# A recurrent block in one planned order on all engines, with eight single-bank PSUM tiles and sigmoids by halves

## The chip, the cores and the metric

The kernel runs on one core of one Trainium2 chip. A core has TensorE (PE in the profile), VectorE (DVE), ScalarE (ACT), GpSimd (POOL) and SyncE (SP), each with a queue of its own that is worked off in order, and 16 DMA engines. SBUF is its working memory; PSUM, which PE writes, is used in banks of 512 float32 for each of 128 partitions, eight in all. The metric is the device time of one execution in microseconds, taken as the median of several runs. A profile records one further execution.

## The reference

One layer of a Griffin-like recurrent block and one of stick-breaking attention, each followed by a SwiGLU feed-forward, on 1024 positions of width 1024. The change touches the recurrent block and the first matmuls after it:

```python
u = jnp.einsum("bsd,de->bse", x, w_in) + b_in
gate_branch, rec = u[..., :LRU_WIDTH], u[..., LRU_WIDTH:]
rec = causal_depthwise_conv(rec, conv_w, conv_b)
gl = jnp.einsum("bsnc,gncd->gbsnd", rec_blk, gate_w).reshape(2, bsz, seq, LRU_WIDTH)
r_gate = jax.nn.sigmoid(gl[0])
i_gate = jax.nn.sigmoid(gl[1])
log_a = -LRU_C * r_gate * jax.nn.softplus(-lam)
a = jnp.exp(log_a)
mult = jnp.sqrt(-jnp.expm1(2.0 * log_a))
b = mult * (i_gate * rec)
_, h = lax.associative_scan(_linear_recurrence_combine, (a, b), axis=1)
y = jax.nn.gelu(gate_branch, approximate=True) * h
return jnp.einsum("bse,ed->bsd", y, w_out) + b_out
```

## The kernel before

Channels lie on partitions, positions in the free dimension, in two halves `n` of 512. Each float32 operand is split into a high and a low part, and each product is three matmuls of 128x128 by 128x512 (`mm3`, L127: high-high, high-low, low-high). A column of `w_in` is one tile of 128 output channels: 8 row tiles times 3 matmuls times 2 halves, 48 matmuls. The recurrent branch has columns A0 to A7, the gate branch B0 to B7, and the gates come in pairs of columns, G0 to G3: for each of two columns and two gates 2 halves of 6 matmuls, again 48.

*The start* (L248 to L323) loads the first four columns in pieces of one row tile (`fr[k]`) beside the input `x` (`xr[k][n]`) and the table of constants `vc`. For each row tile ACT makes the high part of the weights (`fh`) and of the scaled input (`xh`), DVE the low parts (`fl`, `xl`), and PE does half 0 of all four columns `FIRST`. Eight small matmuls on an identity come ahead of them. Then PE does the second halves (`second`, L305), and between them the statistics of the RMSNorm: `column_stats` (L192) sums squares by matmul into one spare bank, DVE and ACT make `rcol`, and `spread` (L172) broadcasts it through the same bank, from where DVE copies it to `rbc[n]`.

*The block* (L326 to L480). A (`stage_a`, L396): DVE scales the column by `rbc` into `u`, ACT applies the newest tap, DVE three more (`rec`), ACT and DVE split the result (`rh`, `rl`). G (`stage_g`, L412): gate matmuls on `rh` and `rl`, then on ACT sigmoids, tanh, exp, sqrt and a copy, and on DVE products and the scan into `ys[e]`. B (`stage_b`, L443): scaling and GELU. Y (L451): `ys[e]` times the GELU. `softplus(-lam)` is a chain of small DVE instructions on 8 elements (L332 to L355). `last_tile` (L455) does column B7, splits all `ys` into `xh` and `xl`, and loads the first tiles of `w_out`. Weights arrive as 512 KB (`raw`, three buffers), ACT copies the high part (`whi`), DVE subtracts the low part (`wlo`).

PSUM is four tiles of two banks (`psl`, two pools). The order of PE in the block is written out by the string of stages; the other engines are ordered there by the framework's scheduler (`manual_schedule` names PE alone, L472). At the start and in the feed-forward the order of every engine is that of the code, but that the scheduler sets the small softplus instructions in between. After the block PE does the output projection (`mix_out_ffn_in`, L541), 16 groups of 24 matmuls into `ob_ps`, in a pool of six single-bank tiles.

## Time and profile before

| what | value |
|---|---|
| median of three runs | 2217.38 us (2214.4 to 2218.05) |
| the profiled execution | 2218.56 us, span 2216.8 |
| PE busy, 0 to 240 us | 229.29 us |
| PE busy, 240 to 300 us | 59.81 us |
| first feed-forward matmul | 330.31 us |

A row of a list by waits reads: engine, tile and line that waited, what ended the wait, time in total, times, longest. A row of a timeline: start, duration, engine, line, operation, output <- inputs, and in brackets the idle time before it. PE's matmuls are pipelined: what counts is how far apart they start, not how long each lasts. A row of a list of windows: the stretch, its length, busy time and count for PE, PE's weight loads, DVE, ACT and POOL, then the granted clock of PE (1.00 is full speed), the share of the DMA engines and GB/s.

### The profile page before, as it was taken

What the parts mean: (1) busy time and instruction counts of PE and PEld (TensorE: products, weight loads), DVE (VectorE), ACT (ScalarE), POOL (GpSimd) and SP (SyncE); (2) the same over time, 40 slices, a digit from 0 to 9 for tenths busy, and PEclk for the clock granted to TensorE, in tenths of its full rate; (3) what the DMA queues carried; (4) which work ended last, traced back from release to release, by engine and by line L of the source; (5) the groups of instructions that cost most, each with busy time, mean ns of one, the idle gap of its engine ahead of it and who ended that gap; (6) DMA issues with size and microseconds to landing.
All of it is one profiled execution on the core that took longest, in us unless ns stands there. A gap on an engine that the chain in (4) does not pass through costs nothing.

```text
span 2216.8 us, 28236 instructions
## 1 busy us (share of the span) xinstructions
PE 2177.2 (98%) x10050; PEld 1805.3 (81%) x10050; DVE 1721.9 (78%) x2412; ACT 1152.7 (52%) x2033; POOL 224.1 (10%) x356
## 2 busy tenths in 40 slices
PE   9899999999999999999999999999999999999997
PEld 7788888888888888878888888878888888888886
DVE  7877778677777887868888888866876777788886
ACT  5657545344444544646666666653534444454455
POOL 0000020000000000003333333421000000000001
PEclk9999999999999999999999999989999999999998
DMA  4021312334444864453333333631133444466442
GB/s 172 10 67 48 124 38 72 105 119 157 143 155 131 278 192 122 145 143 86 88 94 97 104 86 105 186 125 61 46 106 120 152 147 146 145 237 228 126 145 86
DMA packets 132316, 273.50 MB, mean 123 GB/s; under 512 B 15312, under 2 KB 22608, under 8 KB 132176
## 3 DMA queue, kind: packets, MB, share of 16 engines
q1 hardware_dynamic: 131600, 270.86, 38.9%
q8 instruction: 79, 1.29, 0.2%
q10 hardware_dynamic: 576, 0.85, 0.1%
q14 instruction: 61, 0.50, 0.1%
HBM read 175.70 MB, written 70.78 MB: 111 GB/s over the span
## 4 chain that ended last, share of the span: by engine, by line
PE 83%; DVE 9%; ACT 4%; DMA 2%; issue 1%; SPq 1%; DVEq 0%; ACTq 0%
PE p_ps L130 18%; PE p_ps L128 18%; PE p_ps L129 18%; PE qk_ps L130 3%; PE qk_ps L128 2%; PE qk_ps L129 2%; PE ob_ps L129 2%; PE ob_ps L128 2%; PE ob_ps L130 2%; PE wt_ps L1454 2%; PE a_ps L130 2%; PE a_ps L128 2%; PE a_ps L129 2%; DVE F L1442 2%; PE z_ps L1417 1%
## 5 line engine op out<-in xcount | busy, mean ns | idle before, releaser
L1443 POOL TENSOR_TENSOR w<-w,F 128x128 f32<-128x128 f32 (+1 forms) x192 | 184.6, 962 | 314.9 <-DVE F L1440 176.1
L128 PE MATMUL p_ps<-vh,wbh 128*128 128x512 f32 x524 | 204.3, 390 | 2.0 <-ACT ta L1003 2.0
L130 PE MATMUL p_ps<-vh,wcl 128*128 128x512 f32 x524 | 204.2, 390 | 0.5 <-DVE wcl L630 0.5
L130 PE MATMUL p_ps<-vh,wbl 128*128 128x512 f32 x524 | 204.3, 390 | 0.0
L130 PE MATMUL p_ps<-vh,wal 128*128 128x512 f32 x524 | 204.1, 390 | 0.1
L128 PE MATMUL p_ps<-vh,wch 128*128 128x512 f32 x524 | 204.1, 390 | 0.0
L128 PE MATMUL p_ps<-vh,wah 128*128 128x512 f32 x524 | 203.9, 389 | 0.0
L129 PE MATMUL p_ps<-vl,wch 128*128 128x512 f32 x524 | 203.9, 389 | 0.0
L129 PE MATMUL p_ps<-vl,wbh 128*128 128x512 f32 x524 | 203.9, 389 | 0.0
L129 PE MATMUL p_ps<-vl,wah 128*128 128x512 f32 x524 | 203.9, 389 | 0.0
L616 ACT CAST wbh<-sb 128x1024 fp32r<-128x1024 f32 (+2 forms) x69 | 69.6, 1009 | 192.6 <-DVE sb L600 192.6
L1440 DVE TENSOR_TENSOR_SCAN F<-F,unit 128x128 f32<-128x128 f32 (+3 forms) x128 | 126.9, 992 | 5.4 <-ACT F L1436 5.4
L1463 ACT CAST th<-wt_ps 128x512 fp32r<-128x512 f32 x192 | 93.3, 486 | 71.8 <-PE wt_ps L1454 69.8
L1464 DVE TENSOR_TENSOR tl<-wt_ps,th 128x512 fp32r<-128x512 f32 x192 | 105.1, 548 | 28.9 <-ACT th L1463 27.8
L128 PE MATMUL qk_ps<-vh,whi 128*128 128x512 f32 x264 | 118.8, 450 | 0.6 <-ACT vh L208 0.6
L128 PEld LDWEIGHTS p_ps<-vh,wbh 128*128 128x128 f32 x524 | 98.4, 188 | 22.6 <-ACT ta L1003 2.5
L130 PEld LDWEIGHTS p_ps<-vh,wcl 128*128 128x128 f32 x524 | 98.4, 188 | 21.8 <-DVE wcl L630 1.4
L130 PEld LDWEIGHTS p_ps<-vh,wbl 128*128 128x128 f32 x524 | 98.4, 188 | 21.7 <-DVE wbl L620 1.3
L130 PEld LDWEIGHTS p_ps<-vh,wal 128*128 128x128 f32 x524 | 98.4, 188 | 21.4 <-DVE wal L611 1.0
L129 PEld LDWEIGHTS p_ps<-vl,wah 128*128 128x128 f32 x524 | 98.4, 188 | 20.3
L129 PEld LDWEIGHTS p_ps<-vl,wch 128*128 128x128 f32 x524 | 98.4, 188 | 20.3
L128 PEld LDWEIGHTS p_ps<-vh,wah 128*128 128x128 f32 x524 | 98.4, 188 | 20.3
(408 smaller groups left out, 5725.9 us busy)
## 6 DMA issues: line engine op xcount, KB each, us to landing
raw<-in_ffn_w_in SPq DMA_DIRECT2D x88, 512.0 KB, 3.8
vl<-pd SPq DMA_DIRECT2D x128, 256.0 KB, 3.7
pd<-U SPq DMA_DIRECT2D x90, 256.0 KB, 2.3
raw<-in_ffn_w_out SPq DMA_DIRECT2D x28, 512.0 KB, 4.1
raw<-in_attn_w_qkv SPq DMA_DIRECT2D x24, 512.0 KB, 3.6
acc<-pd SPq DMA_DIRECT2D x28, 256.0 KB, 2.6
pph<-rbc SPq DMA_DIRECT2D x28, 256.0 KB, 2.5
ppl<-acc SPq DMA_DIRECT2D x28, 256.0 KB, 2.6
```

The costliest lines, as they stand in the source:

```text
L128: nc.tensor.matmul(ps, lhsT=wh, rhs=mh, start=first, stop=False, **kw)
L129: nc.tensor.matmul(ps, lhsT=wh, rhs=ml, start=False, stop=False, **kw)
L130: nc.tensor.matmul(ps, lhsT=wl, rhs=mh, start=False, stop=last, **kw)
L616: nc.scalar.copy(self.full(self.wb), self.full(self.sb))
L1417: nc.tensor.matmul(ps[:, 0 : c1 - c0], lhsT=lhsT, rhs=KL[q][hx][:, c0:c1], start=False, stop=True)
L1440: nc.vector.tensor_tensor_scan(rev, rev, unit[:, NB - n :][:, ::-1], first, op0=ALU.mult, op1=ALU.add)
L1442: nc.vector.tensor_tensor_scan(rev, rev, rev, first, op0=ALU.mult, op1=ALU.bypass)
L1443: nc.gpsimd.tensor_mul(wt, wt, F[:, 1 : n + 1])
L1454: nc.tensor.transpose(tp[:, c : c + P], W[q, hx, j, kb // 4][:, (kb % 4) * P : (kb % 4 + 1) * P], ident)
L1463: nc.scalar.copy(th[:, q0:], tp[:, q0:])
L1464: nc.vector.tensor_sub(tl[:, q0:], tp[:, q0:], f32(th)[:, q0:])
```

## The change

The recurrent block is emitted by a planner. `lru_plan` enters every step as a task with engine, duration, predecessors and rank; `Plan.emit` always takes the task that can begin first by those durations (ties by rank), and emits it. PE, ACT, DVE and POOL then run in that order. The columns go in another order, PSUM is eight tiles of one bank taken in turn, each half of a column and each half of a gate has its own, and each sigmoid is two instructions of 512. `softplus` moves from the start into the block (`decay`). At the start the table goes first on SP's queue, `xr[0][0]` on ACT's, DVE makes `fh[0]`, there are ten small matmuls, and the second halves stand in whole columns between statistics and spreads. After the block the first four output groups do their first six row tiles, all four, before the last two of each.

```diff
-FIRST = (ND, ND + 1, 0, ND + 2)
+FIRST = (ND, ND + 1, ND + 2, 0)
+class Plan:
+    def __init__(self, **free):
+        self.tasks, self.free = [], free
+
+    def add(self, eng, us, fn, after=(), rank=0, table=None):
+        self.tasks.append((eng, us, fn, [a for a in after if a is not None], rank, table))
+        return len(self.tasks) - 1
+
+    def emit(self):
+        left, end, free, table = set(range(len(self.tasks))), {}, dict(self.free), {}
+        while left:
+            best = None
+            for i in left:
+                eng, us, _, after, rank, tab = self.tasks[i]
+                after[:] = [a if isinstance(a, int) else a[0][a[1]] for a in after]
+                if any(a not in end for a in after):
+                    continue
+                begin = max([free[eng], *(end[a] + (0.0 if self.tasks[a][0] == eng else 0.15) for a in after)])
+                if tab is not None and table.get(eng) != tab:
+                    begin += 1.3
+                key = (begin, rank, i)
+                if best is None or key < best:
+                    best = key
+            begin, _, i = best
+            eng, us, fn, _, _, tab = self.tasks[i]
+            free[eng] = end[i] = begin + us
+            if tab is not None:
+                table[eng] = tab
+            if eng == "dma":
+                free[eng], end[i] = begin + 0.5, begin + us
+            left.remove(i)
+            fn()
+def lru_plan(plan, order, fn):
+    col, rank = 5.44, {w: i for i, w in enumerate(order)}
+    last, end = f"B{ND - 1}", len(order)
+    wants = [w for w in order if w[0] != "Y"][len(FIRST):] + [last, "out0", "out1", "out2"]
+    soft = plan.add("dve", 3.6, fn["soft", 0], [], rank["G0"] - 1)
...
+    def weights(w):
+        i = wants.index(w)
+        r = rank.get(w, end) - 2.5
+        loads[i] = plan.add("dma", 2.6, fn["load", w], [los.get(i - 3), loads.get(i - 1)], r)
+        his[i] = plan.add("act", 1.05, fn["hi", w], [loads[i], his.get(i - 1), used.get(i - 3)], r)
+        los[i] = plan.add("dve", 1.16, fn["lo", w], [his[i]], r)
+        return los[i]
...
+            pe = plan.add("pe", us, fn[key, w, n], [pe, wt, *deps, *free[bank % 8]], r)
+            out.append((pe, bank % 8))
+            bank += 1
...
+    for s_, w in enumerate(order):
+        kind, e = w[0], int(w[1])
+        if kind == "Y":
+            Y[e] = plan.add("dve", 1.16, fn["y", e], [scan[e], gel[e], Y.get(e - 1)], s_ + 3)
+            continue
+        if s_ < len(FIRST):
+            pe = plan.add("pe", col, fn["first", w], [pe], s_)
+            parts = [(None, bank), (pe, bank + 1)]
+            bank += 2
+        else:
+            wt = weights(w)
+        if kind in "AB" and s_ >= len(FIRST):
+            parts = halves(w, wt, (), col, "pe", s_)
+            used[wants.index(w)] = pe
+        if kind == "A":
+            r = rank[f"G{e // 2}"] - 2
+            c = plan.add("dve", 0.1, fn["u", e], [taps.get(e - 2)], r)
+            m = multiply("um", e, parts, r, [c])
+            idn[e] = plan.add("act", 1.24, fn["id", e], [*m, (plus, e - 3) if e > 2 else None, idn.get(e - 1)], r)
+            t = idn[e]
+            for j in range(3):
+                t = plan.add("dve", 1.22, fn["tap", e, j], [t], r)
+            taps[e] = t
+            rh = plan.add("act", 1.05, fn["rh", e], [t, (gates, (e - 3) // 2) if e > 2 else None], r)
+            rl[e] = plan.add("dve", 1.16, fn["rl", e], [rh], r)
...
+                p = [halves((i, g), wt, (rl[2 * e], rl[2 * e + 1]), col / 4, "pg", s_) for g in range(2)]
+                sig = [[], []]
+                for g in range(2):
+                    for n, (q, b) in enumerate(p[g]):
+                        sig[g].append(
+                            plan.add("act", 0.62, fn["sig", i, g, n], [q, scan.get(i - 2), root.get(i - 2), plus.get(i - 2)], r, "sig")
+                        )
+                        free[b] = [sig[g][-1]]
+                ths.append((plan.add("act", 1.15, fn["th", i], [*sig[0], soft], r, "sig"), sig))
+            for i, (th, sig) in zip(pair, ths):
+                r = rank.get(f"Y{i}", end) - 1
+                sr = plan.add("dve", 1.16, fn["sr", i], sig[1], r)
+                t = plan.add("act", 1.15, fn["ex", i], [th], r, "exp")
+                for j in range(3):
+                    t = plan.add("dve", 1.16 if j == 0 else 1.22, fn["m", i, j], [t, sr], r)
+                root[i] = plan.add("act", 1.06, fn["sq", i], [t], r, "sqrt")
+                plus[i] = plan.add("act", 1.05, fn["a1", i], [t], r)
+                st = plan.add("dve", 1.16, fn["st", i], [root[i], sr], r)
+                scan[i] = plan.add("dve", 2.25, fn["scan", i], [st, plus[i]], r)
+                plus[i] = plan.add("act", 0.0, fn["none", 0], [sr, plus[i]], r)
+            used[wants.index(w)] = gates[e] = pe
...
+    turn = [0]
+
+    def ptile(name):
+        turn[0] += 1
+        return psl.tile([P, NB], F32, tag=f"a{(turn[0] - 1) % 8}", name=name)
+
+    pa = {j: [ptile("a_ps") for n in range(NH)] for j in FIRST}
...
-        nc.scalar.dma_start(f4(fr[0]), lru_first[0])
-        nc.scalar.dma_start(vc, table)
+        nc.scalar.dma_start(xr[0][0], x[0, 0])
+        nc.sync.dma_start(vc, table)
         for k in range(ND):
-            nc.sync.dma_start(xr[k][0], x[k, 0])
+            nc.sync.dma_start(f4(fr[k]), lru_first[k])
             if k:
-                nc.sync.dma_start(f4(fr[k]), lru_first[k])
+                nc.sync.dma_start(xr[k][0], x[k, 0])
...
-        for i in range(8):
+        bank = pa[FIRST[3]][1]
+        for i in range(10):
...
-            nc.scalar.copy(fh[k], fr[k])
+            (nc.scalar.copy if k else V.tensor_copy)(fh[k], fr[k])
...
         column_stats(sacc[0], bank, 0)
-        second(0, range(4))
+        second(0, range(ND))
         spread_to(0)
-        second(0, range(4, ND))
-        column_stats(sacc[1], bank, 1)
-        second(1, range(4))
-        spread_to(1)
-        second(1, range(4, ND))
-        second(2, range(ND))
-        second(3, range(ND))
...
+        column_stats(sacc[1], bank, 1)
+        second(1, range(ND))
+        spread_to(1)
+        second(2, range(ND))
+        second(3, range(ND))
...
+        def pe_gate(eg, n):
+            e, g = eg
+            b, c = e // 2, slice(e % 2 * P, (e % 2 + 1) * P)
+            gh, gl = W[f"G{b}"]
+            PS[eg, n] = ptile("g_ps")
+            for k in range(2):
+                q = 2 * b + k
+                mm3(
+                    PS[eg, n], gh[:, g, k, c], gl[:, g, k, c],
+                    half(rech[q], n), half(recl[q], n), k == 0, k == 1,
+                )
...
+        def gate(e, g, n):
+            if g == n == 0:
+                GA[e], GT_[e], GS[e] = wide("ga", 2), wide("gt", 2), wide("gs", 2)
+            nc.scalar.activation(
+                half((GA, GS)[g][e], n), PS[(e, g), n], AF.Sigmoid, bias=col(V_GB + g * ND, e)
+            )
...
-        with tc.manual_schedule(engines={E.PE}):
-            for what in "A0 A1 B0 A2 B1 G0 A3 Y0 Y1 A4 B2 G1 A5 Y2 A6 B3 Y3 G2 A7 B4 Y4 B5 G3 Y5 B6 Y6".split():
...
+        with tc.manual_schedule(engines={E.PE, E.Activation, E.DVE, E.Pool}):
+            plan = Plan(pe=31.2, dve=43.0, act=36.0, dma=20.0)
+            lru_plan(
+                plan,
+                "A0 A1 A2 B0 A3 G0 B1 Y0 Y1 A4 A5 G1 B2 Y2 A6 A7 G2 B3 Y3 B4 Y4 G3 B5 Y5 B6 Y6".split(),
+                Steps(),
+            )
+            plan.emit()
...
+                        if begun or j:
+                            ps = pp.tile([P, NB], F32, tag="p", name="ob_ps")
+                            dense_in(ps, mix.w[d], n)
+                        else:
+                            if k == 0:
+                                four = [pp.tile([P, NB], F32, tag="p", name="ob_ps") for _ in dn]
+                                for t, (d_, n_) in zip(four, dn):
+                                    dense_in(t, mix.w[d_], n_, range(ND - 2))
+                            ps = four[k]
+                            dense_in(ps, mix.w[d], n, range(ND - 2, ND))
```

Bodies of the steps (`u`, `tap`, `scan` and so on) are those of the stages before, one instruction each.

On ACT the program has 28 table loads instead of 35. Three places show the orders.

DVE around the low half of column B2's weights, before (raw_934 is B2's load, raw_866 was A4's, u_851 is A3's, u_921 A4's):

```order
L401 TENSOR_TENSOR u_851<-a_ps_802,rbc0_81 128x512
L439 TENSOR_TENSOR gs_783<-gs_783,gt_782 128x1024
L401 TENSOR_TENSOR u_851<-a_ps_802,rbc1_82 128x512
L440 SCALAR_TENSOR_TENSOR y1_597<-ga_781,gs_783 128x1024
L452 TENSOR_TENSOR y0_596<-y0_596,gb_632 128x1024
L405 SCALAR_TENSOR_TENSOR rec_855<-u_851,vc_80,rec_855 128x1024
L452 TENSOR_TENSOR y1_597<-y1_597,gb_704 128x1024
L405 SCALAR_TENSOR_TENSOR rec_855<-u_851,vc_80,rec_855 128x1024
L401 TENSOR_TENSOR u_921<-a_ps_872,rbc0_81 128x512
L405 SCALAR_TENSOR_TENSOR rec_855<-u_851,vc_80,rec_855 128x1024
L401 TENSOR_TENSOR u_921<-a_ps_872,rbc1_82 128x512
L119 TENSOR_TENSOR wlo_938<-raw_934,whi_936 128x1024
```

and in the change, around the same weights (raw_747; u_796 is A4's, y0 and y1 the first two scans):

```order
L617 TENSOR_TENSOR rl_947<-rec_876,rh_946 128x1024
L538 TENSOR_TENSOR wlo_977<-raw_747,whi_976 128x1024
L630 TENSOR_TENSOR y0_564<-y0_564,gb_709 128x1024
L630 TENSOR_TENSOR y1_565<-y1_565,gb_907 128x1024
L564 TENSOR_TENSOR u_796<-a_ps_878,rbc0_81 128x512
L564 TENSOR_TENSOR u_796<-a_ps_918,rbc1_82 128x512
L561 COPY u_1013<-nbias_459 128x3
L564 TENSOR_TENSOR u_1013<-a_ps_951,rbc0_81 128x512
```

Before, B2's low half stood behind both scans and behind the reads of A4's PSUM. In the change it is still behind the scans, but ahead of the reads of A4; and PE has columns A5 and G1 between A4 and B2.

DVE from the first `rbc` copy, before (cc and ch are the last of the softplus chain):

```order
L353 SCALAR_TENSOR_TENSOR pq_548<-pq_548,kq_546 128x8
L354 TENSOR_SCALAR cc_549<-pq_548 128x8
L355 TENSOR_SCALAR ch_550<-pq_548 128x8
L312 COPY rbc0_81<-a_ps_145 128x512
L196 TENSOR_SCALAR ms_453<-a_ps_145 128x4
```

and in the change between the two `rl` that the first gates read (rl_640 is A0's, rl_681 A1's); the row left out stands for the rest of the softplus chain:

```order
L617 TENSOR_TENSOR rl_640<-rec_600,rh_639 128x1024
L573 SCALAR_TENSOR_TENSOR rec_606<-u_597,vc_80,rec_606 128x1024
L498 SCALAR_TENSOR_TENSOR az_452<-vc_80 128x8
...
L520 TENSOR_SCALAR cc_456<-pq_455 128x8
L521 TENSOR_SCALAR ch_457<-pq_455 128x8
L617 TENSOR_TENSOR rl_681<-rec_606,rh_680 128x1024
L598 TENSOR_TENSOR gb_709<-a_ps_145,rbc0_81 128x512
L598 TENSOR_TENSOR gb_709<-a_ps_146,rbc1_82 128x512
L561 COPY u_712<-nbias_459 128x3
```

The chain has moved from beside the statistics to between the first two `rl`, behind which the reads of B0, A2 and A3 stand.

ACT at the start, with the semaphores that each instruction waits for, before (DMAHW2 is the table's, DMAHW1 `xr[0][0]`'s):

```order
L259 DMA fr_175<-in_lru_first 128x512
L260 DMA vc<-in_table 128x128
L287 ACT_TABLE_LOAD
L287 CAST fh_154<-fr_175 128x512 [waits DMAHW0_49]
L269 ACTIVATE xh_0_88<-xr_0_183,vc 128x512 [waits DMAHW2_49,DMAHW1_49]
```

and in the change (DMAHW1 is the table's, DMAHW0 `xr[0][0]`'s):

```order
L403 DMA xr_0_184<-in_x 128x512
L413 ACT_TABLE_LOAD [waits DMAHW1_49]
L413 ACTIVATE xh_0_88<-xr_0_184,vc 128x512 [waits DMAHW0_49]
L421 ACTIVATE sacc_171<-xr_0_184 128x512
L431 CAST fh_156<-fr_177 128x512 [waits DMAHW3_49]
```

The load of ACT's function table waited for nothing, and now stands behind the wait for the table of constants.

More of the change, by code (lines that the diff above doesn't have):

```diff
@@ new lines, in load, with hi, lo @@
+        def load(w):
+            if w[0] == "o":
+                mix.load(int(w[3]))
+                raws[w] = mix.raw.pop(int(w[3]))
+            elif w[0] == "G":
+                raws[w] = load_raw(lru_gate_w[int(w[1])])
+            else:
+                raws[w] = load_raw(lru_w_in[int(w[1]) + (ND if w[0] == "A" else 0)])
+        def hi(w):
+            W[w] = wtile("whi"), wtile("wlo")
+            nc.scalar.copy(W[w][0], raws[w])
+        def lo(w):
+            h_, l_ = W[w]
+            V.tensor_sub(l_, raws.pop(w), f32(h_))
+            W[w] = tuple((v4 if w[0] == "G" else k3)(t) for t in (h_, l_))
+            if w[0] == "o":
+                mix.w[mix.order[int(w[3])]] = W[w]
@@ new lines, in pe_col @@
+        def pe_col(w, n):
+            PS[w, n] = ptile("a_ps")
+            dense_in(PS[w, n], W[w], n)
+        def pe_gate(eg, n):
[9 more added lines that the diff above has]
+                )
@@ new lines, in u_pad, with u_half, tap3, tap @@
+        def u_pad(e):
+            U[e] = lp.tile([P, S + 16], F32, tag="u", name="u", bufs=2)
+            V.tensor_copy(U[e][:, 0:3], nbias[:, e, 0:3])
+        def u_half(e, n):
+            V.tensor_mul(U[e][:, 3 + n * NB : 3 + (n + 1) * NB], PS[f"A{e}", n], rbc[n])
+        def tap3(e):
+            rec[e] = wide("rec", 3)
+            nc.scalar.activation(
+                rec[e], U[e][:, 3 : S + 3], AF.Identity, bias=cb[:, e : e + 1], scale=col(V_CW + 3 * ND, e)
+            )
+        def tap(e, j):
+            V.scalar_tensor_tensor(
+                rec[e], U[e][:, j : j + S], col(V_CW + j * ND, e), rec[e], op0=ALU.mult, op1=ALU.add
+            )
```

256 lines of the change are left out of this document (131 added, 125 removed).

## The prediction

> **What bounds the kernel now.** I read the page first, for what sets the end, then windows for where that engine is not at work, then its waits, then its order of time around them.
>
> ```profile
> span 2216.8 us, 28236 instructions
> PE 2177.2 (98%) x10050; PEld 1805.3 (81%) x10050; DVE 1721.9 (78%) x2412; ACT 1152.7 (52%) x2033; POOL 224.1 (10%) x356
> ...
> 100.00:120.00 20.00, 14.44 (x52) 11.32 (x52) 18.21 (x18) 5.93 (x6) 0.00 (x0) 0.83 0.24 80
> 120.00:240.00 120.00, 120.00 (x531) 99.43 (x530) 89.55 (x83) 88.42 (x82) 0.00 (x0) 1.00 0.15 44
> ```
>
> PE is busy for 98% of the span, so only its idle time and its slow time can be won. In the recurrent block that time lies in one stretch, 100 to 120: PE 14.44 of 20, its granted clock 0.83 instead of 1.00, and DVE 18.21 of 20. PE's waits up to 300 us say what ended them.
>
> ```profile
> PE a_ps L130 <- DVE wlo L119: 5.6, 1, 5.6
> PE a_ps L129 <- DVE xl L272: 1.6, 1, 1.6
> PE a_ps L175 <- DVE rcol L170: 1.2, 1, 1.2
> ...
> 103.90 0.39 PE L129 MATMUL a_ps<-xl,whi 128*128 128x512 f32 x1
> 109.84 0.79 PE L130 MATMUL a_ps<-xh,wlo 128*128 128x512 f32 x1 [5.56 <-DVE wlo L119]
> ...
> 115.56 0.43 PE L128 MATMUL a_ps<-xh,whi 128*128 128x512 f32 x1
> ...
> 244.82 0.39 PE L128 MATMUL ob_ps<-xh,whi 128*128 128x512 f32 x1
> ...
> 246.87 0.39 PE L128 MATMUL ob_ps<-xh,whi 128*128 128x512 f32 x1
> 247.45 0.50 PE L129 MATMUL ob_ps<-xl,whi 128*128 128x512 f32 x1 [0.19 <-DVE xl L467]
> ```
>
> The long wait is for `wlo`, the low half of column B2's weights. The ten matmuls from 244.82 to 246.87 start (246.87 - 244.82) / 9 = 0.228 us apart, which is PE's pace. The wait was no lack of data, as ACT and DVE show:
>
> ```profile
> 93.35 1.04 ACT L115 CAST whi<-raw 128x1024 fp32r<-128x1024 f32 x1
> 98.74 0.69 DVE L401 TENSOR_TENSOR u<-a_ps,rbc 128x512 f32<-128x512 f32 x1
> 99.34 2.28 DVE L440 TENSOR_TENSOR_SCAN y<-ga,gs 128x1024 f32<-128x1024 f32 x1
> 108.57 1.22 DVE L119 TENSOR_TENSOR wlo<-raw,whi 128x1024 fp32r<-128x1024 f32 x1
> ```
>
> The high half was there at 93.35 + 1.04 = 94.39; the low half stood in DVE's queue behind scans, products and taps until 108.57. So the order on DVE sets this loss, and an order is what the change gives.
>
> **The change, part by part.** *The wait in the block.* From 103.90 to 109.84 PE needed 0.228 and took 5.94, 5.71 too many. The 13 matmuls from 109.84 to 115.56 took 5.72 instead of 13 x 0.228 = 2.96, 2.76 too many, at the lower clock that the idle time left behind. Both go if no new wait comes: 8.47 us.
>
> B2 now comes later in PE's order. Between the first gates (G0) and B2, PE had G0, A3 and A4, and has G0, B1, A4, A5 and G1. A column is 48 matmuls, 48 x 0.228 = 10.9 us, a gate pair the same: 54.7 us of cover instead of 32.8. In DVE's new queue the low half of B2 stands ahead of the first read of column A4, when PE still has A5 and G1 before it, 21.8 us. The other columns' weights lie as far ahead. The cover is thinnest at G0, so I walk DVE's queue there, from the copy of `rbc1`, with durations of before:
>
> ```profile
> 39.05 0.69 DVE L312 COPY rbc<-a_ps 128x512 f32<-128x512 f32 x1 [0.48 <-PE a_ps L175]
> 38.12 0.17 DVE L353 SCALAR_TENSOR_TENSOR pq<-pq,kq 128x8 f32<-128x8 f32 x1
> 38.33 0.17 DVE L354 TENSOR_SCALAR cc<-pq 128x8 f32<-128x8 f32 x1
> L405 DVE SCALAR_TENSOR_TENSOR rec<-u,vc,rec 128x1024 f32<-128x1024 f32 x24 | 30.5, 1282 | 0.2
> ```
>
> The copy 0.69, four halves of `u` 4 x 0.69 = 2.8, one `wlo` 1.22, six taps 6 x 1.28 = 7.7 (the row of 24, mean 1282 ns), two `rl` of `wlo`'s shape 2.44, and the decay constants, moved here from the start: 34 tiny instructions that feed each other, 38.33 - 38.12 = 0.21 apart, 7.1. Together 22.0 us, at most: successive rows start closer than they last (98.74 to 99.34 is 0.60, for 0.69). PE meanwhile does two half columns and A3, 96 x 0.228 = 21.9, and four matmuls of G0 before it needs the second `rl`: 22.8. Margin 0.8 to about 2.5 us. The eighth group of G0 needs the bank that `u`'s second half of A3 frees: by then PE has 21.9 + 42 x 0.228 = 31.5, and DVE 22.0 plus six halves 4.1, a `wlo` 1.22, three taps 3.85 and one product of `wlo`'s shape 1.22, 32.4 at most. That is 0.9 late at worst and 1 to 2 early if rows start as closely as shown. I take no wait, the starts shown being nearer, and keep 0.9 for the range. Queued behind these rows on DVE are the gate products and scans, for which PE waits only through the last eight row tiles, and the weights: from the second `rl` to B2's low half DVE has 8 halves, 22 full-width rows and 2 scans, 5.5 + 28.2 + 4.6 = 38.3 us, and PE 54.7 - 0.9 = 53.8. The 15 us between them are there for DVE's own waits on ACT.
>
> *Sigmoids by halves, eight banks.* ACT gains 16 instructions, at 0.72 for a half (`xh`, quoted below) 11.5 us at most, and loses 7 table loads of 1.28, 9.0. The 2.5 us between them vanish in its idle time, 31.6 of the 120 us from 120 on; with that cover gone PE would pay the 2.5. Half tiles free each bank after a half read instead of a whole one, which can only be earlier; no wait of PE in the list above was for a bank, so I count no gain.
>
> *Spread and statistics.* All of column A0's second half now comes ahead of the first spread, so the wait for `rcol` goes. But the second statistics write the bank that the copy to `rbc` reads, and follow at once:
>
> ```profile
> 36.30 0.40 PE L130 MATMUL a_ps<-xh,fl 128*128 128x512 f32 x1
> 37.85 1.16 PE L175 MATMUL a_ps<-ident,rcol 128*128 128x128 f32 x8 [1.16 <-DVE rcol L170]
> 38.77 0.48 PE L128 MATMUL a_ps<-xh,fh 128*128 128x512 f32 x1
> ```
>
> Removed: 37.85 - 36.30 - 0.23 = 1.32. Added: the copy ended at 39.05 + 0.69 = 39.74, where PE went on at 38.77: 0.97, with a hand-over of 0.05 1.02. Net 0.30 won.
>
> *The start.* The table now goes first on SP's queue and `xr[0][0]` first on ACT's.
>
> ```profile
> 1.17 0.46 ACTq L260 DMA_DIRECT2D vc<-in_table  x1
> 1.66 1.28 ACT L287 ACT_TABLE_LOAD   x1 [1.66 <-PEq L1620]
> 4.51 0.62 ACT L287 CAST fh<-fr 128x512 fp32r<-128x512 f32 x1 [1.57 <-DMA fr<-in_lru_first]
> 5.43 0.72 ACT L269 ACTIVATE xh<-xr,vc 128x512 fp32r<-128x512 f32 x1 [0.30 <-DMA vc<-in_table]
> 0.74 0.87 SPq L262 DMA_DIRECT2D xr<-in_x  x2
> 5.36 0.17 DVE L332 SCALAR_TENSOR_TENSOR az<-vc 128x8 f32<-128x8 f32 x1 [5.36 <-DMA vc<-in_table]
> 7.77 0.75 DVE L272 SCALAR_TENSOR_TENSOR xl<-xr,vc,xh 128x512 fp32r<-128x512 f32 x1
> 8.57 0.80 PE L129 MATMUL a_ps<-xl,fh 128*128 128x512 f32 x1 [1.58 <-DVE xl L272]
> 13.34 0.40 PE L128 MATMUL a_ps<-xh,fh 128*128 128x512 f32 x1
> ```
>
> The table landed 5.36 - 1.17 = 4.19 after its issue; issued at 0.74 it lands at 4.93. ACT's function table load, free at 1.66 before, now stands behind the wait for it: 4.93 + 1.28 = 6.21. Then `xh` 0.72 to 6.93, `xl` 0.75, and two hand-overs of 0.05: PE's second matmul at 7.78 instead of 8.57, 0.79 won. `fh` and `fl` are off this path: `fr[0]`, landed by 4.51, moves one issue (0.46) back on another queue, and two DVE instructions under 0.75 end by 6.5, since the tiny ones that stood ahead of `fl` (from 5.36 on) are gone. The next pair (`fr[1]`, `xr[1]`) is one issue later too; PE needs it 11 slow matmuls after its second. Bounds: with the table no earlier than 5.36, 0.36 won; landing as fast as `fr`, near 4.5, 1.2.
>
> *The end.* Four output tiles now begin with the first six of eight row tiles, so 72 matmuls cover the last two columns: 247.45 - 246.87 - 0.23 = 0.35 won. Their sums reach DVE up to 54 x 0.228 = 12.3 us later, with four of six banks held; the fifth and sixth tile take the free two, and PE needs the sums only in the feed-forward stage, some 80 us on.
>
> **Sum.** 8.47 + 0.30 + 0.79 + 0.35 = 9.91 us off the profiled execution's 2218.56 (span 2216.8 and 1.8 around it): 2208.6. That execution lies 1.18 above the median 2217.38, so the forecast is 2207.5.
>
> **Rivals.** *The clock rises before the first column.* The start held 11 slow steps from 8.57 to 13.34, 4.77 us where 11 x 0.228 = 2.5 would do. Ten warm-up matmuls instead of eight keep PE at work longer:
>
> ```profile
> 1.36 3.78 PE L285 MATMUL a_ps<-ident 128*128 128x128 f32 x16 [1.36 <-POOL ident masks.py:199]
> ```
>
> Eight took 3.78, ten take 4.7. If that is enough, 2.3 more are won: 2205.2. Against it: PE then idles about a microsecond before its data, and eight were not enough in the one execution shown; I give it one in five. The Trainium skill ("TensorE: Matmul & The Clock Gate", Part 1) says that the clock doubles after one fully busy window of about 3.4 us whose phase is free; that agrees with the slow 5.72 us behind the wait, and by it, as an estimate, ten hold a whole window in (4.7 - 3.4) / 3.4 = 0.38 of executions and eight in 0.11.
>
> *DVE is late at G0.* If its queue runs 2 to 3 us behind my walk (the decay rows are the likeliest reason, 7.1 us), PE idles that long, below the 5.56 that cost clock: 2210.5.
>
> *The wait only moves.* The plan's durations are estimates, and if another column's weights or `rl` come as late as B2's did, the 8.47 return: 2216.0. For it: the plan counts 3.6 for the decay rows that I put at 7.1. Against it: 20 us of cover.
>
> *Half clock in the gates, the slower side.* Each gate group is 6 matmuls, 1.37 us, and now waits for a bank of its own, freed by ACT's half sigmoids and DVE's halves. Were PE to stop at most groups, the clock could fall and a pair of gates would run at the slow step, (13.34 - 8.57) / 11 = 0.434: 48 x (0.434 - 0.228) = 9.9 more for each of four. One such pair brings the kernel level with before, 2217.4; from two on it is slower, 2227.3. Against it: from 120 to 240, with three gate pairs, PE was busy 120.00 of 120 at clock 1.00. The Trainium skill (same page, "A second HAM failure mode: psum-queue depth-cycling") tells of a kernel where turning through banks did this; no row here shows it.
>
> **How the numbers follow.** The forecast has 0.57, the early clock 0.20, DVE late 0.13, the wait moved 0.06, half clock 0.04. 0.2% is 4.4 us, about what a measurement of this kernel tells from no change. The first three lie beyond it: faster 0.90, same 0.06, slower 0.04. The range goes from 2203.5 (early clock, and runs 1.7 apart from their median) to 2212.0 (DVE late, with the start's worse bound and the 0.9 at the eighth group).
>
> **What would show it.** Right: no PE wait over 1.1 us between 20 and 250; granted clock 1.00 in every 20 us there; a wait of about 1 us for the `rbc` copy near 39; PE's second column matmul near 7.8; the first feed-forward matmul some 10 us earlier. Wrong: a PE wait for `rl` or `u` near 70 to 80, one for `wlo` in any column, gate matmuls 0.43 apart, or a later stage that gives the time back.

## The result, and the profile after

| | before | changed |
|---|---|---|
| median, us | 2216.74 (4 runs, 2214.4 to 2218.05) | 2202.87 (4 runs, 2201.98 to 2205.54) |
| ratio to before | | 0.9941, 95% interval 0.9923 to 0.9958 |
| profiled execution, us | 2218.56 | 2203.10 |
| first feed-forward matmul, us | 330.3 | 316.5 |

The change is 13.9 us faster in the median, where 9.9 was forecast. As a time, 2202.87 lies 4.6 below the forecast and 0.6 below the low end of the range; 0.64 of both is the kernel before itself, whose median fell from 2217.38 to 2216.74 with a fourth run. The page of the changed kernel, its windows in the stretch that held the loss before, and PE's waits up to 330 (line waited for: us in total, times, longest):

```profile
span 2201.3 us, 28255 instructions
PE 2169.1 (99%) x10054; PEld 1799.9 (82%) x10054; DVE 1726.9 (78%) x2413; ACT 1146.2 (52%) x2041; POOL 225.3 (10%) x356
```

```profile
100.00:120.00 20.00, 20.00 (x90) 16.56 (x89) 16.55 (x17) 10.47 (x13) 0.00 (x0) 1.00 0.16 54
120.00:140.00 20.00, 20.00 (x90) 16.54 (x89) 17.41 (x15) 13.79 (x14) 0.00 (x0) 1.00 0.17 53
```

```profile
PE a_ps L429 <- POOL ident masks.py:199: 1.4, 1, 1.4
PE a_ps L334 <- DVE rbc L456: 0.8, 1, 0.8
```

From 100 to 120 PE goes from 14.44 busy at clock 0.83 to 20.00 at 1.00. Of six waits up to 330 two are left, one of them for the identity matrix at the very start. The order of time shows what became of B2's weights and of the thin place at G0:

```profile
63.94 1.22 DVE L617 TENSOR_TENSOR rl<-rec,rh 128x1024 fp32r<-128x1024 f32 x1
67.21 0.39 PE L269 MATMUL g_ps<-rl,whi 128*128 128x512 f32 x1
74.31 0.68 DVE L564 TENSOR_TENSOR u<-a_ps,rbc 128x512 f32<-128x512 f32 x1
75.82 0.39 PE L268 MATMUL g_ps<-rh,whi 128*128 128x512 f32 x1
103.27 1.22 DVE L538 TENSOR_TENSOR wlo<-raw,whi 128x1024 fp32r<-128x1024 f32 x1
121.16 0.39 PE L270 MATMUL a_ps<-xh,wlo 128*128 128x512 f32 x1
```

The row at 103.27 is B2's low half (the seventh `wlo` on DVE, as B2 is the seventh column or gate pair behind the first four). It ends at 104.49 and PE reads it at 121.16, 16.7 us later, where before it came 5.56 too late. At G0 the second `rl` ends at 65.16 and is read at 67.21 (2.05 ahead); the eighth gate group's bank is free at 74.99 and taken at 75.82 (0.83 ahead). The start:

```profile
0.74 0.39 SPq L404 DMA_DIRECT2D vc<-in_table  x1
...
3.44 1.28 ACT L413 ACT_TABLE_LOAD   x1 [3.44 <-DMA vc<-in_table]
4.28 0.43 DVE L431 CAST fh<-fr 128x512 fp32r<-128x512 f32 x1 [4.28 <-DMA fr<-in_lru_first]
4.74 0.72 ACT L413 ACTIVATE xh<-xr,vc 128x512 fp32r<-128x512 f32 x1
5.49 0.75 DVE L416 SCALAR_TENSOR_TENSOR xl<-xr,vc,xh 128x512 fp32r<-128x512 f32 x1
5.65 0.77 PE L268 MATMUL a_ps<-xh,fh 128*128 128x512 f32 x1
6.30 0.52 PE L269 MATMUL a_ps<-xl,fh 128*128 128x512 f32 x1
...
8.98 0.39 PE L268 MATMUL a_ps<-xh,fh 128*128 128x512 f32 x1
```

The table landed 3.44 - 0.74 = 2.70 after its issue, where 4.19 was reckoned. PE's second column matmul came at 6.30 instead of 8.57, and the 11 steps behind it took 2.68 instead of 4.77. At the first spread:

```profile
34.97 1.05 PE L315 MATMUL a_ps<-ident,rcol 128*128 128x128 f32 x8
36.80 1.05 PE L334 MATMUL a_ps<-ones,sacc 128*128 128x1 f32 x8 [0.78 <-DVE rbc L456]
```

The wait for `rcol` is gone, and the forecast wait for the copy to `rbc` is there with 0.78. The two kernels can be compared at the first feed-forward matmul, which came 330.3 - 316.5 = 13.8 us earlier; 2.27 of these are the second column matmul, 2.09 the steps behind it, and 9.4 lie later. The profiled executions differ by 15.5; the last 1.7 arise in code behind that matmul which the change doesn't touch.

### The profile page after: what moved, and what is told of

It is laid out like the page before. It is cut to its first block, busy times and chain, and to the rows that moved or that the text cites. A ratio compares the mean times of both kernels' runs of the same rounds, so it can differ in the third digit from the quotient of the medians.

```text
span 2201.3 us, 28255 instructions
## 1 busy us (share of the span) xinstructions
PE 2169.1 (99%) x10054; PEld 1799.9 (82%) x10054; DVE 1726.9 (78%) x2413; ACT 1146.2 (52%) x2041; POOL 225.3 (10%) x356
## 4 chain that ended last, share of the span: by engine, by line
PE 87%; DVE 8%; ACT 3%; issue 1%; DMA 1%; SPq 0%; DVEq 0%; POOL 0%; ACTq 0%; POOLq 0%
PE p_ps L270 18%; PE p_ps L268 18%; PE p_ps L269 18%; PE a_ps L268 3%; PE a_ps L269 3%; PE a_ps L270 3%; PE qk_ps L270 3%; PE qk_ps L268 3%; PE qk_ps L269 3%; PE ob_ps L268 2%; PE ob_ps L269 2%; PE ob_ps L270 2%; PE wt_ps L1634 2%; DVE F L1622 2%; PE z_ps L1597 1%
## 5 line engine op out<-in xcount | busy, mean ns | idle before, releaser
L269 PEld LDWEIGHTS p_ps<-vl,wbh 128*128 128x128 f32 x524 | 98.7, 188 | 20.4
```

The lines of the kernel that those rows point to most:

```text
L269: nc.tensor.matmul(ps, lhsT=wh, rhs=ml, start=False, stop=False, **kw)
```

## The experiments

The times of the twelve kernels below are medians of four to twelve runs, and a ratio is to the kernel before, run beside each. The runs of one kernel lie within 1.4 to 8.1 us of each other, the longer ones mostly with a lower mean granted clock. So time differences under some 3 us are not leant on, and the place of the first feed-forward matmul in the profile is given beside them.

**The block alone, with the start of before** (DMAs, `fh[0]` on ACT, eight warm-up matmuls and the interleaved spread as before):

```diff
...
-        for i in range(10):
+        for i in range(8):
...
-            (nc.scalar.copy if k else V.tensor_copy)(fh[k], fr[k])
+            nc.scalar.copy(fh[k], fr[k])
...
-        second(0, range(ND))
+        second(0, range(4))
         spread_to(0)
+        second(0, range(4, ND))
...
```

> The changed kernel with the start of before: order of the first DMAs, ACT makes fh[0], eight warm-up matmuls, second() and spread() interleaved in the two first columns; the planned order of the block, the half sigmoids and the eight banks stay. Theory (8.47 of the gain is the wait for B2's wlo and the slow clock behind it, 0.35 the end, the rest the start): PE's second column matmul near 8.5 as in before, the first steps about 0.43 apart, and then no wait of PE over 1.6 us between 40 and 320; the first feed-forward matmul near 330.31 - 8.47 - 0.35 = 321.5 against 330.31 before and 316.54 in the changed kernel; some 9 us faster than before. Rival (the start, with the clock high from its first step, brings most of it, and the block merely moves waits): a wait of 5 us or more stays between 80 and 250, and less than 5 us is won.

Measured: 2205.39, ratio 0.9949 (0.9936 to 0.9962); first feed-forward matmul 318.1. PE's waits, and rows of its start:

```profile
PE a_ps L315 <- DVE rcol L310: 1.9, 1, 1.9
PE a_ps L429 <- POOL ident masks.py:199: 1.4, 1, 1.4
PE a_ps L268 <- ACT xh L413: 0.9, 1, 0.9
PE a_ps L269 <- DVE xl L416: 0.3, 1, 0.3
```

```profile
5.99 0.75 DVE L416 SCALAR_TENSOR_TENSOR xl<-xr,vc,xh 128x512 fp32r<-128x512 f32 x1 [0.50 <-ACT xh L413]
6.80 0.50 PE L269 MATMUL a_ps<-xl,fh 128*128 128x512 f32 x1 [0.29 <-DVE xl L416]
...
9.45 0.39 PE L268 MATMUL a_ps<-xh,fh 128*128 128x512 f32 x1
```

No wait stands behind 40 (the last, for `rcol`, ends at 34.72), so the block's gain does not come from the start. The matmul came 12.2 earlier, more than the 8.8 expected, and the surplus is in the start that was put back: `xl` now starts at 5.99 instead of 7.77, as the decay rows that stood ahead of it on DVE are in the plan. PE's second column matmul is 1.77 earlier, the 11 steps take 2.65 (2.12 less), the wait for `rcol` is 0.76 longer: 12.2 - 1.77 - 2.12 + 0.76 = 9.1 for block and end, against 8.47 + 0.35.

**The start alone**, in the kernel before (the same edits the other way):

```diff
-        nc.scalar.dma_start(f4(fr[0]), lru_first[0])
-        nc.scalar.dma_start(vc, table)
+        nc.scalar.dma_start(xr[0][0], x[0, 0])
+        nc.sync.dma_start(vc, table)
...
```

> The kernel before with the start of the changed kernel: order of the first DMAs, fh[0] on DVE, ten warm-up matmuls, the second halves whole ahead of each spread; the block in the scheduler's order with two-bank PSUM tiles and whole sigmoids. Theory: PE's wait of 5 to 6 us for B2's wlo and the 13 slow matmuls behind it stay; the second column matmul comes at 6.3 to 8, later than in the changed kernel if the decay constants stand ahead of xl on DVE; 1 to 4.4 us faster than before (4.36 where the clock is high from the first step). Rival (the block's wait is a consequence of the late start): the wait for wlo shrinks below 2 us and 8 us or more are won.

Measured: 2213.72, ratio 0.9988 (0.9980 to 0.9997); first feed-forward matmul 327.6, 2.7 earlier. The longest of PE's waits, and the windows around 40:

```profile
PE a_ps L130 <- DVE wlo L119: 5.6, 1, 5.6
...
PE a_ps L175 <- DVE rcol L170: 1.2, 1, 1.2
PE a_ps L194 <- DVE rbc L312: 0.8, 1, 0.8
```

```profile
35.00:40.00 5.00, 3.04 (x20) 2.34 (x19) 2.40 (x17) 0.31 (x2) 0.00 (x0) 0.96 0.14 58
40.00:45.00 5.00, 5.00 (x17) 3.98 (x16) 0.83 (x5) 0.10 (x1) 0.00 (x0) 0.70 0.00 0
```

The wait for `wlo` stays whole, so the rival falls. Part of the 4.0 us won at the start (the second column matmul at 6.68 and 11 steps in 2.66) is given back: the wait for `rcol` stays, the one for `rbc` joins it, and behind both the clock was 0.70 from 40 to 45.

**Eight warm-up matmuls** in the changed kernel (`range(10)` to `range(8)`):

> The changed kernel with eight warm-up matmuls instead of ten. In the changed kernel's profile the first 11 column steps took 2.68 us (6.30 to 8.98) where before took 4.77. Theory A (the count raised the clock): with eight the first 11 steps take 4.5 to 4.8 us again and the time is about 2 us longer in most runs. Theory B (the earlier data did, since PE idles less ahead of the first column): the steps still take about 2.7 us and the time is within 0.5 us of the changed kernel. Theory C (the phase of the clock's window against the start is free): runs scatter by about 2 us with both counts, with a mean some 0.5 us longer with eight.

Measured: 2204.0 (2201.35 to 2205.98), ratio 0.9941 (0.9929 to 0.9952). In the profile the 11 steps took 2.66 (6.22 to 8.88). So ten are not needed for it, against A. B and C are left: all fourteen profiled executions, one of each kernel here, fit B. The two in which PE stood longest for the first `xl` (before, 1.58, and the scheduler with new columns below, 1.88) took 4.77 and 4.22 for these steps; the twelve in which it stood 0.64 or less took 2.61 to 2.97, with eight or ten. Two slow ones are few, and C is not excluded.

**The columns as before, planned**, and **the new columns, scheduled**. The first gives the planner the old order of columns, the second the kernel before the new one:

```diff
-FIRST = (ND, ND + 1, ND + 2, 0)
+FIRST = (ND, ND + 1, 0, ND + 2)
...
-                "A0 A1 A2 B0 A3 G0 B1 Y0 Y1 A4 A5 G1 B2 Y2 ...
+                "A0 A1 B0 A2 B1 G0 A3 Y0 Y1 A4 B2 G1 A5 Y2 ...
```

> The changed kernel's planner with the order of columns and gates of before (A0 A1 B0 A2 B1 G0 A3 ... B2 G1 ...) and the order of row tiles that goes with it; everything else as changed. It tells whether the planned order on DVE alone takes the wait for B2's wlo away, or whether PE needs the 54.7 us of cover (instead of 32.8) between G0 and B2. Theory as forecast (the order on DVE sets the loss, the columns' cover gives it room): with 32.8 us of cover and 38.3 us of DVE's work from G0's second rl to B2's wlo a planner that keeps all of it ahead would be 5 us late; one that puts wlo ahead of scans and taps can be in time, so a wait of 0 to 2 us for wlo and 0 to 3 us slower than the changed kernel. Rival (the cover is what matters, not who orders DVE): waits of 4 us or more and a slow stretch come back, 6 to 9 us slower than the changed kernel.

> The kernel before with the new order of columns and gates (A0 A1 A2 B0 A3 G0 B1 ...) and of row tiles; DVE and ACT stay in the scheduler's order, PSUM stays four tiles of two banks, sigmoids stay whole. Theory (DVE's order set the loss, but the cover alone helps too): the wait of 5.6 us for B2's wlo goes or shrinks below 2 us, and another wait of 1 to 5 us may come where the scheduler puts a weight or rl behind scans; 3 to 8 us faster than before. Rival (cover alone suffices, the planner and the eight banks bring nothing): no PE wait over 1.2 us from 40 to 250 and 8 to 9 us faster than before, level with the changed kernel but for its start. Rival (the planned order is all): a wait of 5 us or more stays, within 2 us of before.

Measured: 2201.8 planned with old columns (2201.11 to 2202.92), ratio 0.9936 (0.9923 to 0.9948), first feed-forward matmul 316.7; 2207.56 scheduled with new ones, ratio 0.9962 (0.9949 to 0.9974), 321.0. B2's low half and its reader, planned with old columns:

```profile
81.04 1.23 DVE L538 TENSOR_TENSOR wlo<-raw,whi 128x1024 fp32r<-128x1024 f32 x1 [0.74 <-ACT whi L534]
...
99.38 0.39 PE L270 MATMUL a_ps<-xh,wlo 128*128 128x512 f32 x1
```

and all of PE's waits up to 330, scheduled with new columns:

```profile
PE a_ps L129 <- DVE xl L272: 1.9, 1, 1.9
PE a_ps L175 <- DVE rcol L170: 1.6, 1, 1.6
PE a_ps L285 <- POOL ident masks.py:199: 1.4, 1, 1.4
PE a_ps L128 <- ACT xh L269: 0.8, 1, 0.8
```

With the cover of before, 32.8 us, the plan has the low half ready 99.38 - 82.27 = 17.1 ahead. With the scheduler's own order on DVE and ACT, whole sigmoids and two-bank tiles, the new columns remove the wait as well: the rival holds that their cover alone suffices. So each part alone is enough. The 8.47 are not a sum of the two: the change has both where one would do. The two edited lines of the column order even have the block's whole gain without the planner, since the 4.5 us between 321.0 and the changed kernel's 316.5 lie ahead of the block but for 0.1: 3.6 up to the matmul 11 steps behind the second (12.57 and 8.98), and 0.8 in the wait at the first spread (1.61 for `rcol` and 0.78 for `rbc`).

**Two-bank tiles with whole sigmoids**, and **two-bank tiles with half sigmoids**, planned (the edits of the planner and of the sigmoid itself are left out here):

```diff
...
-        return psl.tile([P, NB], F32, tag=f"a{(turn[0] - 1) % 8}", name=name)
+        i = (turn[0] - 1) % 8
+        if i % 2 == 0:
+            two_banks[0] = psl.tile([P, S], F32, tag=f"a{i // 2}", name=name)
+        return half(two_banks[0], i % 2)
...
```

> The changed kernel with PSUM as four tiles of two banks and a sigmoid over both halves of a gate at once, in the planner and the code; the rest as changed. Theory (halves and eight banks cost and gain nothing, since no wait of PE was for a bank): within 0.5 us of the changed kernel, no new wait of PE over 1 us. Rival (each half in its own bank is what lets the gates go on at G0): PE waits 0.7 us or more for a bank at the fourth gate pair of G0 or at the columns behind it, and 1 to 8 us are lost, the more if the wait costs the clock.

> The changed kernel with PSUM as four tiles of two banks, but sigmoids by halves as changed; in the plan both banks come free when both halves are read. wide_gates, which had whole sigmoids as well, lost about 7 us: PE waited 1.17 and 1.09 for rl at 111.94 and 189.52 and 3.06 for a bank that a whole sigmoid held at 202.84, and ran slow behind it. Theory A (the banks: a tile of two is free only when both halves have been read): a wait of 1 us or more for a bank stays, and 3 to 8 us are lost against the changed kernel. Theory B (the sigmoids: a whole one starts later and holds ACT longer): no wait for a bank over 0.5 us, and within 1.5 us of the changed kernel.

Measured: whole 2209.72, ratio 0.9971 (0.9960 to 0.9982), first feed-forward matmul 325.1; half 2205.38, ratio 0.9957 (0.9944 to 0.9969), 320.5. PE's longest waits in the block, whole and then half:

```profile
PE a_ps L268 <- ACT ga L590: 3.1, 1, 3.1
PE g_ps L269 <- DVE rl L621: 2.3, 2, 1.2
```

```profile
PE g_ps L271 <- DVE rl L624: 2.1, 1, 2.1
...
PE g_ps L270 <- DVE u L571: 0.5, 1, 0.5
```

The forecast counted no gain for these parts, and that falls. Whole sigmoids in two-bank tiles put PE 8.6 us back at the first feed-forward matmul, half sigmoids in two-bank tiles 4.0. With whole ones the wait of 3.06 is for a bank, at 202.84 and not at G0, with a clock of 0.66 from 203 to 208 behind it; those of 1.17 and 1.09 for `rl` cost no clock. Of A and B neither holds alone: with halves the wait for a bank is only 0.5 (the eighth gate group of G0, where the margin was 0.83), but an `rl` comes 2.15 late at 190. The plan is made anew for each. The scheduled kernel with the new columns had whole sigmoids in two-bank tiles and no wait in the block; so it is the planned order that needs the halves and the banks, and which of its steps does is open.

**The first four output tiles whole** (each with all eight row tiles at once):

```diff
...
-                            if k == 0:
-                                four = [pp.tile([P, NB], F32, tag="p", name="ob_ps") for _ in dn]
-                                for t, (d_, n_) in zip(four, dn):
-                                    dense_in(t, mix.w[d_], n_, range(ND - 2))
-                            ps = four[k]
-                            dense_in(ps, mix.w[d], n, range(ND - 2, ND))
+                        ps = pp.tile([P, NB], F32, tag="p", name="ob_ps")
+                        dense_in(ps, mix.w[d], n)
```

> The changed kernel with the first four output tiles done whole instead of their first six of eight row tiles first. Theory: 36 matmuls fewer cover the last two columns' scans, products and splits, so the wait of before for xl (0.19) comes back and 0.2 to 0.4 us are lost. Rival (in the new order the last columns are later against PE, so the cover carries more): 0.5 to 3 us lost, in a wait of the first output tiles for xh or xl of the last column. Rival (nothing needs it): within 0.2 us.

Measured: 2207.07, ratio 0.9959 (0.9945 to 0.9973); first feed-forward matmul 323.3. PE in order of time, and its windows there:

```profile
234.23 0.50 PE L268 MATMUL ob_ps<-xh,whi 128*128 128x512 f32 x1 [0.52 <-ACT xh L632]
236.07 0.50 PE L269 MATMUL ob_ps<-xl,whi 128*128 128x512 f32 x1 [1.33 <-DVE xl L633]
237.32 0.80 PE L268 MATMUL ob_ps<-xh,whi 128*128 128x512 f32 x1 [0.53 <-ACT xh L632]
238.47 0.80 PE L269 MATMUL ob_ps<-xl,whi 128*128 128x512 f32 x1 [0.36 <-DVE xl L633]
```

```profile
235.00:240.00 5.00, 3.05 (x7) 1.82 (x8) 4.38 (x8) 2.17 (x4) 0.00 (x0) 0.72 0.33 93
240.00:245.00 5.00, 5.00 (x15) 3.95 (x14) 0.49 (x1) 0.00 (x0) 0.00 (x0) 0.60 0.90 308
```

The first rival holds in its place and goes past its 3 us. PE begins the output at 229.5, where before it began at 242.8, and DVE's last two `xl` of the block run from 237.74 to 239.25; four waits of 2.74 together and a slow stretch behind them cost 4.2 us in the median (6.8 in this execution). So in the planned order the split of the first four tiles carries 4.2 us of the gain into the next stage. The scheduled kernel with the new columns began the output at 234.0, has no split, and its list above shows no wait there.

**A second chain of tiny rows at G0** (34 instructions ahead of the decay constants, into tiles that nothing reads):

```diff
+            V.scalar_tensor_tensor(az2, lam, -1.0, lam, op0=ALU.mult, op1=ALU.max)
...
+            for cf in (1.0 / 5040, 1.0 / 720, 1.0 / 120, 1.0 / 24, 1.0 / 6, 0.5, 1.0) * 4:
+                V.scalar_tensor_tensor(pq2, pq2, cf, gq2, op0=ALU.add, op1=ALU.mult)
```

> The changed kernel with 34 more tiny instructions on DVE (a second chain as long as the decay constants', into tiles of its own that nothing reads) ahead of the decay constants at G0; they last about 0.2 us each, some 7 us. It tests whether G0 is where the plan is thinnest. In the changed kernel the second rl of G0 ended 2.05 us before PE used it, and the eighth gate group's bank came free 0.83 us before its turn. Theory: PE waits about 7 - 2 = 5 us for rl near 67, runs slow behind it for up to 3.4 us, and 5 to 8 us are lost. Rival (DVE has room there, the rows are hidden): less than 1 us lost.

Measured: 2210.66, ratio 0.9970 (0.9958 to 0.9982); first feed-forward matmul 325.5. Of the waits and windows:

```profile
PE g_ps L269 <- DVE rl L627: 4.7, 1, 4.7
```

```profile
65.00:70.00 5.00, 2.21 (x10) 1.49 (x8) 4.18 (x26) 1.05 (x1) 0.00 (x0) 1.00 0.00 0
70.00:75.00 5.00, 3.04 (x7) 2.47 (x8) 4.90 (x14) 0.60 (x1) 0.00 (x0) 0.63 0.01 2
75.00:80.00 5.00, 5.00 (x17) 3.87 (x17) 4.93 (x5) 4.17 (x6) 0.00 (x0) 0.69 0.34 105
```

The second `rl` of G0 ends 6.75 later (at 71.91 instead of 65.16); less the margin of 2.05 that makes the wait of 4.7. Behind it PE's matmuls stood 0.43 apart until 78.1, some 6 us, 3.0 more than at full pace. The two make 7.7, and 7.8 were lost in the median. G0 is as thin as walked.

**The statistics later**, to take out the last wait but that for the identity matrix:

```diff
+        second(1, range(2))
         column_stats(sacc[1], bank, 1)
-        second(1, range(ND))
+        second(1, range(2, ND))
```

> The changed kernel with the second column_stats put behind the first six matmuls of the second column's second half instead of right behind the first spread. Theory (in the changed kernel PE stood 0.78 for the copy to rbc at 36.80, since the statistics write the bank that the copy reads): that wait goes, none takes its place, and the first feed-forward matmul comes 0.8 us earlier, near 315.7; the time falls by as much, less than these runs can tell. Rival (rcol for the second spread becomes late instead): a wait of 0.5 us or more at the second spread.

Measured: 2200.86 (2200.35 to 2203.26), ratio 0.9931 (0.9918 to 0.9943), first feed-forward matmul 315.8. PE's only wait up to 330 is the one for the identity matrix. The theory holds in the profile; it is the lowest median of the kernels run, by less than the times can tell.

**The function table early**, in a tile of one column and then in one of 16 (`[P, 16]`, its first column written):

```diff
+        nc.scalar.copy(cp.tile([P, 1], F32, name="early"), ones)
...
+            if k == 0:
+                x_lo(k, 0)
             nc.vector.tensor_sub(fl[k], fr[k], f32(fh[k]))
-            x_lo(k, 0)
+            if k:
+                x_lo(k, 0)
```

> The changed kernel with a copy of one column of ones on ACT ahead of its first use of the constants' table, so that ACT's function table load no longer stands behind the wait for the table's landing (3.44 in the changed kernel), and xl ahead of fl in DVE's queue for the first piece of x. Theory (the load's 1.28 us stand on the path to xh): xh starts near 3.5 instead of 4.74, PE's first column matmul near 4.7 instead of 5.65 where fh is there, and the second at 5.0 to 5.4 instead of 6.30; 0.9 to 1.3 us faster than the changed kernel if the clock is high from the first step as there. Rival 1 (fh on DVE, a cast of 0.43 from 4.28, sets the first matmul): 0.2 to 0.9 us faster. Rival 2 (columns starting sooner meet the low clock, or the next piece of x or of the filter sets the pace): no gain, or up to 2 us slower.

> table_early again, with its one new tile made 16 columns wide (64 bytes a partition) instead of one column; the instructions are the same. table_early's one-column tile takes 32 bytes in SBUF, so every tile placed behind it begins 32 bytes past a multiple of 64, and its matmuls of 128x512 came about 0.2335 us apart from 60 on instead of 0.2275 (88 instead of 90 in 20 us), which made it some 30 us slower than the changed kernel. Theory (it is the place of the moving operand in SBUF): with 64 bytes the step is 0.2275 again and the time falls to that of the changed kernel or up to 0.5 us below, since the start was won nothing there (first column matmul 5.65 in both, third 6.65 and 6.66). Rival (it is the early table load, or ACT's or DVE's order at the start): the step stays near 0.2335 and the time near 2235.

Measured: 2235.4, ratio 1.0086 (1.0073 to 1.0099), with one column; 2227.18, ratio 1.0046 (1.0033 to 1.0060), with 16. Nothing was won at the start. With one column `xh` ran from 3.65 and `fh[0]` was made by 4.75, but PE's first column matmul came at 5.65 as in the changed kernel, without a wait:

```profile
1.36 4.64 PE L430 MATMUL a_ps<-ident 128*128 128x128 f32 x20 [1.36 <-POOL ident masks.py:199]
...
5.65 0.77 PE L268 MATMUL a_ps<-xh,fh 128*128 128x512 f32 x1
```

It followed straight on the ten warm-up matmuls (20 in the record), so these set the start there, and not `fh` as rival 1 had it. And PE was slower all through. One window of the feed-forward stage, of the changed kernel, of one column and of 16:

```profile
500.00:700.00 200.00, 200.00 (x884) 165.66 (x883) 144.37 (x189) 83.67 (x127) 0.00 (x0) 1.00 0.44 142
```

```profile
500.00:700.00 200.00, 200.00 (x867) 162.41 (x866) 143.84 (x189) 82.56 (x125) 0.00 (x0) 1.00 0.45 143
```

```profile
500.00:700.00 200.00, 200.00 (x869) 162.73 (x868) 141.15 (x185) 81.75 (x124) 0.00 (x0) 1.00 0.45 144
```

PE is busy for 200 of 200 at clock 1.00 in all three, and does 884, 867 and 869 matmuls. The theory that 64 bytes cure it falls as it was put. The two experiments differ in the width of one tile alone, and from 100 to 300 did 859 and 876 matmuls (885 in the changed kernel), so that width does bear on PE's step. What it changes in the program is where other tiles lie: `xh` and many more begin on a multiple of 128 bytes of their partition in the changed kernel, 32 bytes past one with one column, 64 past with 16. But the place of a matmul's own operands is not the whole cause. In the first feed-forward stage, up to 900, some three in five of the matmuls read tiles that begin on such a multiple in all three programs. Where one of these follows another they start 0.230 and 0.2315 apart on average, with one column and with 16, and 0.2265 in the changed kernel. So the cause is open, and whether the early load has a part in it was not tried: the same copy into a tile that exists would tell.

## Why the prediction was right, and where it was off

- **The wait in the block, 8.47: right in place, kind and size.** Wait and slow clock are gone, nothing took their place, and block and end together measure 9.1 in the block alone, against 8.82. The cover came out as walked: from the second `rl` to the end of B2's low half DVE took 104.49 - 65.16 = 39.3, where 38.3 was reckoned, and PE 121.16 - 67.21 = 54.0, where 53.8 was. The reason was half of it: "the order on DVE sets this loss" was told together with the columns' cover as one cause, but each alone takes the loss away, and the new columns do so with DVE's order left to the scheduler.
- **G0: right.** The margins of 0.8 to 2.5 and of -0.9 to 2 measured 2.05 and 0.83, and the doubled chain shows the price beyond the first.
- **Spread and statistics, 0.30: right.** 1.32 went, and 0.78 of wait came instead of 0.97, so some 0.5 was won.
- **The end, 0.35: right against before, wrong as a measure of what the edit does.** The term asked what the 0.19 wait of before cost; in the planned order the same edit holds back 2.74 of waits and the slow clock, 4.2 us.
- **Sigmoids by halves and eight banks, 0: wrong in its reason.** "No wait of PE in the list above was for a bank" was read from before's order. In the planned order 6.9 us depend on them, with margins down to 0.83. That the zero fits the sum is luck: the planned order brings the need, and the change has both halves and banks to meet it.
- **The start, 0.79: the step that was mis-sized.** Two terms. The table was reckoned to land 4.19 after its issue, as it did behind `fr[0]` on ACT's queue; first on SP's it took 2.70, and these 1.49 are what separates 7.78 from 6.30. And the 11 steps behind it ran at full pace, 2.09 more. That outcome was the rival put at one in five, but not by its mechanism: eight warm-up matmuls give it too where `xl` is early, and the slow steps go with a wait for `xl` of 1.58 or more. That wait came with the decay rows ahead of `xl` on DVE. The sum had seen them go, without asking what PE's idle time there did to the clock, as it had asked at 109.84. As far as two slow starts tell, that is the step; that the low end of the range, taken from that rival, came within 0.6 is luck in the same way.

0.79 + 1.48 + 2.09 = 4.4 for the start and 9.4 for the rest make the 13.8 of the profile, and the 9.4 are near 8.47 + 0.5 + 0.35. The slow stretch of the scheduled kernel with new columns, eight steps of 0.43 from 8.35 to 11.82, is 3.5 us long. The Trainium skill ("TensorE: Matmul & The Clock Gate", Part 1) names a window of about 3.4 us for the clock, whose phase it calls free. The stretch of 3.5 agrees with it, that of before (8.57 to 13.34) is longer, and whether the outcome of a start hangs on that phase no run here shows.

## What to carry to other kernels

A wait of PE can cost twice, as idle time and as slow clock behind it. Here the waits of 3 us or more were all followed by a slow stretch. Of the shorter ones those of 1.58 and 1.88 at the start were, and so were those that stood close together (1.17 and 0.78; the four of 2.74), while single ones of 1.1 to 2.2 later on were not. So both costs belong in a term's range, at the start too. When two parts of a change each give an engine more room, test each alone before calling their sum the cause. Test a part with no visible gain by taking it out of the new kernel, since margins there differ from those of the old one. After adding even a tiny tile, count PE's matmuls in a stage that the edit doesn't touch.

## What was not expected of the hardware

- With one more tile of one column, and the edits beside it, PE does 867 matmuls in 200 us instead of 884, at clock 1.00 and without a wait, and 32.5 us are lost in all; with 16 columns 24.3. The cause is open.
- A transfer of the same table landed 2.70 after its issue as the first of its queue, and 4.19 as the second behind `fr[0]`.
- The start's slow steps of before (0.434 apart from 8.57 to 13.34) stand under a granted clock of 1.00 in the record; with the new columns scheduled the same kind of steps stand under a lower one (0.91 over the first 20 us). So the pace has to be read there from the steps and not from that record.
